# Joining two value products into one of 512 columns, squaring half rows in another order, and a place of its own for one tile of Fourier rows

## The chip, the core and the metric

The kernel runs on one core of a Trainium2 chip. The metric is the device time of one execution in microseconds (us), the median of several runs. The engines are named as the profile names them: PE (TensorE matmul) and PEld (its weight load), DVE (VectorE), ACT (ScalarE), POOL (GpSimd) and SP (SyncE, which here only issues DMAs). Instructions of one engine run in the order in which they stand in its queue.

## The reference, cut to what matters

One encoder layer for 512 + 256 tokens of width 2048: an RMS norm, an input projection, two groups of heads (a Fourier mix and windowed attention), an output projection, a squared-ReLU MLP and a last norm. What this case touches:

```python
h = rmsnorm(x, ln_mix_g)
z = h @ w_in                       # columns: 1024 Fourier | 1024 q | 256 k | 256 v
v = z[..., o3:].reshape(B, S, N_KV_HEADS, HEAD_DIM)
of = fourier_mix(zf, w_fourier).reshape(B, S, F_WIDTH)
mixed = concatenate([rmsnorm(of, out_norm_fourier_g), rmsnorm(oa, out_norm_attn_g)], -1)
x = x + mixed @ w_out
```

The inputs and results are float32.

## The kernel before, in words

**Products in parts.** Every float32 operand is split into a high and a low part (`split`, L66: ACT copies the source into the rounded high part, DVE subtracts it from the source for the low part), and a product is the sum of three matmuls: high by high, high by low, low by high.

**The value stage (L473 to L606)** is the first of the kernel. It makes v = x w for all 768 tokens (six tiles `m` of 128 rows) with 256 columns of `w_in[9]`, over 16 slices `k` of 128. `prepare(c)` scales and splits the x and w of one chunk: six chunks of one slice, then five of two slices. `v_term(c, m, term, i)` (L539) issues one matmul: stationary is a 128x128 block of x, moving are 256 columns of w, and the three terms of a tile add up in the first 256 columns of its PSUM bank `pv[m]`. The halves of w lie in two tiles, `whl[..][0]` (high) and `whl[..][1]` (low). In the last chunk the order is by tile, so that `pv[0]` is done first; `v_keep(m)` (L559) then splits `pv[m]` from PSUM into `vhl`, ACT first and DVE after it.

In the same stage `half_load(i)` (L548) reads six half rows of x (`halves[0]` to `halves[5]`, tiles named `xt`, 1024 columns each), and `half_square(i)` (L553) squares one on ACT and keeps its sum. Three of the six, 0 to 2, are squared after `high7(0)` and `high7(1)` and ahead of the six `v_keep`, the others, 3 to 5, after them. DVE has, in its order: `low7(0)`, `low7(1)`, two `xsum` (L404), the six subtractions of `v_keep`.

**The seven-product stage (L654 on)** follows at once. `product7(n)` (L276) issues 24 matmuls of 384 columns (L287) on weights which `load7(n)` (SP, L238) reads, `high7(n)` (ACT, L265) rounds and `low7(n)` (DVE, L273) completes; for each block of weights the third matmul is the first to use the low part. Products 0 and 1 use weights prepared in the value stage. `load7(2)` is the first to read into a tile named `wr`, and `high7(2)` stands on ACT right behind the squares of `halves`. Product 0 writes the PSUM banks of `pv[0]` and `pv[1]`, so it waits for the last reader of `pv[0]`.

**Where tiles lie.** The value stage's pool `xp` is closed before the pool `hq` of the next stage opens, and `hq` gets the same bytes of SBUF. A load into a new tile waits for the last instruction that reads or writes an old tile under it. In KB per partition from the start of both pools, as the program of the kernel before places them:

| pool | tile and place |
|---|---|
| `xp` | `wv[0..3]` 0-4, 12-16, 8-12, 4-8; `vt` 16-28 |
| `xp` | `halves[0]` 28-32, `[1]` 48-52, `[2]` 44-48, `[3]` 40-44, `[4]` 36-40, `[5]` 32-36 |
| `hq` | `ws` 0-24, `d7` 24-30, `z10` 30-34.5, `z01` 34.5-43.5 |
| `hq` | `wr` of `load7(2)` 43.5-47.5, of `load7(4)` 51.5-55.5, of `load7(6)` 47.5-51.5 |

**The Fourier rows.** `of_d` in DRAM holds the result of the Fourier group. `load_of(m)` (L180, its DMA L189) reads the 1024 rows of one tile m of tokens, `split_of(m)` (L1222) splits them for the output projection, and `proj_slot` (L1235) multiplies: 8 steps of k for each tile m, interleaved with attention by an order written out by hand. In that part `at(t, fn)` puts work at a step (slot m begins at 8 m), and the constants `t_...` (L1182 to L1186) are such steps. Before it, `after(piece, fn, place)` (L909) puts work behind a piece of the last input product (`pz`, L1001). `load_of(0)` reads early, into two tiles of the pool `kq2`; `load_of(1)` (L1248) stands behind the last piece and reads into the place of a later tile in the pool `op`, under which tiles of the pz stage lie.

Of the kernel before, what the change touches and what calls it, by code (L numbers as in the profile page):

```python
# [11 lines left out]
F32 = mybir.dt.float32  # L12
F32R = mybir.dt.float32r
BF16 = mybir.dt.bfloat16
AF = mybir.ActivationFunctionType
ALU = mybir.AluOpType
# [4 lines left out]
P = 128  # L21
# [4 lines left out]
NM = T // P  # L26
NK = D // P
# [4 lines left out]
NKV = 4  # L32
# [8 lines left out]
def hybrid_encoder(ctx: ExitStack, tc: tile.TileContext, a: dict):  # L41
    nc = tc.nc
# [156 lines left out]
    with ExitStack() as ph:  # L199
# [273 lines left out]
        with tc.tile_pool(name="xp", bufs=1, reuse_waits="tile") as xp, tc.manual_schedule(  # L473
            engines={mybir.EngineType.SP, mybir.EngineType.Activation, mybir.EngineType.DVE}
        ):

            wv = [xp.tile([P, 4, 256], F32, tag="raw", name="raw", bufs=4) for _ in range(4)]
            whl = [[wpool.tile([P, 4, 256], F32R, tag=t, name=t, bufs=4) for t in ("wh", "wl")] for _ in range(4)]
            flat = xs[1][:].rearrange("p o k t -> p (o k t)").rearrange("p (s o t) -> p s o t", s=8, o=2)
            vt = xp.tile([P, 4, 2, HALF], F32R, tag="vt", name="vt")  # L480
            room = [flat[:, 0:4], flat[:, 4:8], vt[:]]
            chunks = [(k, 1) for k in range(6)] + [(k, 2) for k in range(6, NK, 2)]
            homes = [(k // 4, k % 4) for k in range(6)] + [(1, 2), (2, 0), (0, 0), (1, 0), (2, 0)]
            xhl = {}

            def load_x(k0, n):
                for t in range(2):
                    nc.sync.dma_start(xr[k0 // 8][t][:, k0 % 8 : k0 % 8 + n, :], a["x_t"][:, t, k0 : k0 + n, :])

            def load_wv(k0, n, queue=nc.sync):  # L490
                queue.dma_start(wv[k0 // 4][:, k0 % 4 : k0 % 4 + n, :], w_in[9][:, k0 : k0 + n, :])

            def prepare(c):

                k0, n = chunks[c]
                r, s0 = homes[c]
                ks = slice(k0 % 8, k0 % 8 + n)
                raw = [xr[k0 // 8][t][:, ks, :] for t in range(2)]
                rows = [room[r][:, s0 + i * n : s0 + i * n + n] for i in range(2 if k0 >= 8 else 1)]
                if k0 < 8:  # L500
                    parts = [[xs[0][:, o, ks, :] for o in range(2)]]
                else:
                    parts = []
                parts += [[x[:, :, o, :] for o in range(2)] for x in rows]
                xhl[c] = parts
                w, wk = k0 // 4, slice(k0 % 4, k0 % 4 + n)
                wh, wl = (x[:, wk, :] for x in whl[w])
                gb = g0[:, k0 : k0 + n].rearrange("p (k o) -> p k o", o=1).to_broadcast([P, n, HALF])
                gain = lambda t: nc.vector.tensor_tensor(out=raw[t], in0=raw[t], in1=gb, op=ALU.mult)
                first = 1 if n == 1 else 0  # L510
                scaled = lambda k, out, x: nc.scalar.activation(out, x, AF.Copy, scale=g0[:, k : k + 1])
                if n == 1:
                    split(wh, wl, wv[w][:, wk, :])
                if c < 2:
                    for t in range(2):
                        split(*parts[t], raw[t], g0[:, k0 : k0 + 1])
                    return
                if n == 1:
                    scaled(k0, parts[0][0], raw[0])
                    gain(0)  # L520
                for i in range(n):
                    scaled(k0 + i, raw[first][:, i], raw[first][:, i])
                if n == 1:
                    nc.vector.tensor_tensor(out=parts[0][1], in0=raw[0], in1=f32(parts[0][0]), op=ALU.subtract)
                    split(*parts[1], raw[1])
                else:
                    gain(1)
                    split(wh, wl, wv[w][:, wk, :])
                    for t in range(2):
                        split(*parts[t], raw[t])  # L530
                if 6 <= c < 8:
                    k = c - 6
                    x, y = (xr[0][t][:, k, :] for t in range(2))
                    scaled(k, x, x)
                    nc.vector.tensor_scalar(out=y, in0=y, scalar1=g0[:, k : k + 1], scalar2=None, op0=ALU.mult)

            pv = [pp.tile([P, 512], F32, tag="x", bufs=6, name="pv") for m in range(NM)]

            def v_term(c, m, term, i):  # L539
                k0, n = chunks[c]  # L540
                l, r = ((0, 0), (0, 1), (1, 0))[term]
                k = k0 + i
                nc.tensor.matmul(  # L543
                    pv[m][:, :256], xhl[c][m // 3][l][:, i, m % 3 * P : (m % 3 + 1) * P], whl[k // 4][r][:, k % 4, :],
                    start=(k == 0 and term == 0), stop=(k == NK - 1 and term == 2),
                )

            def half_load(i):  # L548
                m, h = divmod(i, 2)
                halves[i] = xp.tile([P, 1024], F32, tag="xt", name="xt", bufs=6)[:]  # L550
                nc.sync.dma_start(halves[i], x_rows(m)[:, h * 1024 : (h + 1) * 1024])

            def half_square(i):  # L553
                m, h = divmod(i, 2)
                nc.scalar.activation(halves[i], halves[i], AF.Square, accum_out=ssq[:, 4 * m + h : 4 * m + h + 1])

            halves = {}

            def v_keep(m):  # L559
                split(vhl[:, m, :, 0, :], vhl[:, m, :, 1, :], pv[m][:, :256].rearrange("p (g d) -> p g d", g=NKV))  # L560

            pw = pp.tile([P, 512], F32, tag="t", bufs=2, name="pw")

            def warm(n):
                for _ in range(n):
                    nc.tensor.matmul(pw[:, :P], ones[:], ones[:], start=True, stop=True)

            warm(9)
            nc.scalar.dma_start(gall[:], a["gains"])
            nc.scalar.activation(mhalf[:, 7:8], mhalf[:, 7:8], AF.Copy)  # L570
            for k, n in ((0, 1), (1, 2), (3, 2), (5, 2), (7, 1), *((k, 2) for k in range(8, NK, 2))):
                if k % 2 == 0:
                    load_wv(k, 2)
                load_x(k, n)
                if k in (1, 3, 5):
                    load_wv(k + 1, 2)
            for i in range(2):
                half_load(i)
                load7(i)
            for i in range(2, 6):  # L580
                half_load(i)
            for c, (k0, n) in enumerate(chunks):
                prepare(c)
                if c + 1 < len(chunks):
                    order = [(term, m) for term in range(3) for m in range(NM)]
                    if n == 1:
                        order.sort(key=lambda x: (x[1] // 3, x))
                    for term, m in order:
                        for i in range(n):
                            v_term(c, m, term, i)  # L590
                else:
                    for n2 in range(2):
                        high7(n2)
                        low7(n2)
                    for i in range(3):
                        half_square(i)
                    for m in range(NM):
                        for term in range(3):
                            for i in range(n):
                                v_term(c, m, term, i)  # L600
            for n in range(2):
                xsum(b11, b12, b11, n)
            for m in range(NM):
                v_keep(m)
            for i in range(3, 6):
                half_square(i)  # L606

        def row_load(i):
# [234 lines left out]
        kt = {}  # L843
# [65 lines left out]
        def after(piece, fn, place=6):  # L909
            todo.setdefault(piece, []).append((place, len(todo[piece]), fn))  # L910
# [50 lines left out]
        after(7.5, close_folds, 7)  # L961
        after(8.5, close_fourier, 7)
        after(9, lambda: load_of(0, [kt["kq2"].tile([P, 4, P], F32, tag="ofr", name="ofr", bufs=2) for _ in range(2)]), 7)
        after(9, lambda: load_q(1), 8)
        after(10.5, lambda: load_q(2), 8)
        after(9, negate_sink, 8)
# [216 lines left out]
    t_trans, d_trans, t_th, t_tl, t_pv, d_pv, t_ob, t_os, t_put = 9.2, 1.05, 1.2, 1.4, 16.2, 0, 0.5, -0.6, 2.2  # L1183
    t_w, t_of, t_xc, t_y, t_oa, t_oa0, t_oa1, t_lq = 42.05, 7.45, -0.05, 2.7, 67, 4.2, 4.95, 1.5
    t_low = {2: 3.3}
    t_sq, t_red, t_w3, d_w, t_of1, t_of2, t_lof, t_la = 6.7, 7.9, 0.5, 2.15, 3, 6.5, 15.2, 1  # L1186
    events, clock = [], [0.0, 0]

    def at(t, fn):
# [55 lines left out]
                    nc.tensor.matmul(ps, ll(kk), pieces[kk // 2][0][:, kk % 2, :], start=False, stop=False)  # L1245
            step(k)

    load_of(1)  # L1248
    ofs = [[op.tile([P, FG, P], F32R, tag=f"of{c}{m}", name=f"of{c}{m}") for c in "hl"] for m in range(NM)]
    at(-2, lambda: split_of(0))  # L1250
    at(t_w3, lambda: out_split(3, False))
# [771 lines left out]
```

## Time and profile before

| | before |
|---|---|
| median of 3 runs | 2564.15 us (2563.36 to 2564.28) |
| the profiled execution, its time | 2563.83 us |
| its span in the profile | 2562.0 us |
| PE busy | 2552.0 us of the span |
| DVE / ACT / POOL busy | 1810.6 / 1127.7 / 272.6 us |
| mean granted clock of PE | 0.999 |

The profile shows one execution of 2563.83 us. Its rows begin with a start in us from the start of the span and a duration; several alike in a row are grouped as xN with the time from the first start to the last end. In square brackets stands the idle time before an instruction and what ended it. A matmul's duration contains its way through the array, so what one costs in a row of them is the distance from start to start.

### The profile page before, as it was taken

Reading aid. Unit: us, or ns where it says so; the run is one execution under the profiler, and the core shown is the slowest. Engines: PE = TensorE matmul, PEld = TensorE weight load, DVE = VectorE, ACT = ScalarE, POOL = GpSimd, SP = SyncE. Lnnn points to the kernel's source line nnn. Section 1 sums busy time; section 2 is a strip of 40 time slices with the busy share of each in tenths; the row PEclk is TensorE's granted clock in tenths of the full one; section 3 lists DMA queues with packets and bytes.
Section 4 is the critical chain, followed back from the end, with each engine's and each line's share of the span. In section 5 each row is a group of like instructions: output and inputs, shape, how many; then the busy total and the mean of one; then the engine's idle time right before and its main releaser. Section 6 shows DMA issues by size and latency. Waiting matters only on the chain.

```text
span 2562.0 us, 34695 instructions
## 1 busy us (share of the span) xinstructions
PE 2552.0 (100%) x13415; PEld 2336.7 (91%) x13415; DVE 1810.6 (71%) x2144; ACT 1127.7 (44%) x1630; POOL 272.6 (11%) x387
## 2 busy tenths in 40 slices
PE   9999999999999999999999999999999999999998
PEld 9999998888899999999999999988888888888887
DVE  7877767678466556556777777667766756777687
ACT  7454557674233333334445454433333333333335
POOL 0023333223201010100000000200000000000000
PEclk9999999999999999999999999999999999999999
DMA  7686386465745444466666666775543662554364
GB/s 294 229 285 214 115 245 193 138 179 187 236 163 186 159 165 163 165 207 225 231 230 214 217 215 216 277 279 176 176 146 124 221 222 89 176 183 157 101 211 153
DMA packets 261029, 496.99 MB, mean 194 GB/s; under 512 B 21147, under 2 KB 145569, under 8 KB 260737
## 3 DMA queue, kind: packets, MB, share of 16 engines
q1 hardware_dynamic: 193600, 332.00, 40.7%
q10 hardware_dynamic: 51360, 101.43, 10.5%
q0 software_dynamic: 15904, 61.36, 7.1%
q8 instruction: 105, 1.72, 0.3%
q14 instruction: 60, 0.48, 0.1%
HBM read 373.19 MB, written 121.51 MB: 193 GB/s over the span
## 4 chain that ended last, share of the span: by engine, by line
PE 98%; DMA 1%; DVE 0%; ACT 0%; issue 0%; POOL 0%; SPq 0%; ACTq 0%; DVEq 0%; POOLq 0%
PE pu L1390 36%; PE pd L1825 35%; PE pm L1243 10%; PE p L287 7%; PE pz L1001 3%; PE pv L543 1%; PE o L1122 1%; PE s L1045 1%; PE t L1100 1%; PE pa L796 0%; PE ptx L138 0%; PE pe L815 0%; DMA ofd<-of 0%; DMA raw<-in_w_out 0%; DMA xr<-in_x_t 0%
## 5 line engine op out<-in xcount | busy, mean ns | idle before, releaser
L1390 PE MATMUL pu<-xf,wh 128*128 128x384 f32 x3072 | 780.2, 334 | 0.0
L1390 PEld LDWEIGHTS pu<-xf,wh 128*128 128x128 f32 x3072 | 554.1, 188 | 1.5 <-ACT o L1408 1.3
L1825 PE MATMUL pd<-wh,sh 128*128 128x512 f32 x1332 | 517.7, 389 | 0.0
L1825 PE MATMUL pd<-wl,sh 128*128 128x512 f32 x1332 | 517.7, 389 | 0.0
L1825 PE MATMUL pd<-wh,sl 128*128 128x512 f32 x1332 | 517.5, 389 | 0.0
L1390 PE MATMUL pu<-xf,wl 128*128 128x384 f32 x1536 | 513.1, 334 | 0.0
L1802 ACT ACTIVATE wh<-rd 128x1024 fp32r<-128x1024 f32 x200 | 202.4, 1054 | 522.3 <-PE pd L1825 424.4
L1812 DVE TENSOR_TENSOR wl<-rd,wh 128x1024 fp32r<-128x1024 f32 x200 | 236.1, 1221 | 226.2 <-ACT wh L1802 225.5
L1370 ACT ACTIVATE wh<-ur 128x1024 fp32r<-128x1024 f32 x160 | 170.1, 1063 | 382.6 <-PE pu L1390 226.7
L1825 PEld LDWEIGHTS pd<-wl,sh 128*128 128x128 f32 x1332 | 250.0, 188 | 51.9
L1825 PEld LDWEIGHTS pd<-wh,sh 128*128 128x128 f32 x1332 | 250.0, 188 | 51.9
L1825 PEld LDWEIGHTS pd<-wh,sl 128*128 128x128 f32 x1332 | 249.9, 188 | 51.8 <-DVE sl L1813 0.3
L1390 PEld LDWEIGHTS pu<-xf,wl 128*128 128x128 f32 x1536 | 288.3, 188 | 0.0
L1376 DVE TENSOR_TENSOR wl<-ur,wh 128x1024 fp32r<-128x1024 f32 x160 | 195.5, 1222 | 76.1 <-ACT wh L1370 76.1
L1411 DVE TENSOR_TENSOR o<-pu,o 128x768 f32<-128x768 f32 x160 | 152.9, 956 | 122.4 <-PE pu L1390 114.9
L287 PE MATMUL p<-xs,wh 128*128 128x384 f32 x672 | 170.6, 334 | 0.0
L1795 DVE TENSOR_TENSOR rd<-rd 128x1024 f32<-128x1024 f32 x112 | 131.7, 1217 | 0.0
L1390 PE MATMUL pu<-xs,wh 128*128 128x384 f32 x512 | 129.8, 334 | 0.0
L1370 ACT ACTIVATE wh<-sx 128x1024 fp32r<-128x1024 f32 x64 | 67.9, 1062 | 130.5 <-PE pu L1390 104.3
L287 PEld LDWEIGHTS p<-xs,wh 128*128 128x128 f32 x672 | 121.4, 188 | 0.1
L287 PE MATMUL p<-xs,wl 128*128 128x384 f32 x336 | 112.2, 334 | 0.0
L1813 DVE TENSOR_TENSOR sl<-sr,sh 128x768 fp32r<-128x768 f32 x111 | 105.6, 951 | 0.0
(309 smaller groups left out, 3774.9 us busy)
## 6 DMA issues: line engine op xcount, KB each, us to landing
rd<-in_w_down SPq DMA_DIRECT2D x176, 512.0 KB, 5.2
ur<-in_w_up SPq DMA_DIRECT2D x128, 512.0 KB, 3.8
sr<-sd SPq DMA_DIRECT2D x95, 384.0 KB, 5.4
pd<-o ACTq DMA_DIRECT2D x60, 384.0 KB, 2.3
o<-pd POOLq DMA_DIRECT2D x60, 384.0 KB, 6.2
sd<-sm ACTq DMA_DIRECT2D x60, 384.0 KB, 2.8
raw<-in_w_in SPq DMA_DIRECT2D x40, 512.0 KB, 5.1
raw<-in_w_out SPq DMA_DIRECT2D x32, 512.0 KB, 4.5
```

The lines of the kernel that those rows point to most:

```text
L287: nc.tensor.matmul(ps7[own, g, r][:, :HALF], l[:, i, r * P : (r + 1) * P], x[:, o, 4 * e + i, :], start=(opens and e == 0 and i == 0 and q ...
L1001: nc.tensor.matmul(ps[c][s][:, :HALF], w[:, i, cs], whole[j // 2][s][o][:, 4 * (j % 2) + i, :], start=first and n == 0, stop=stop and n == 2,)
L1243: nc.tensor.matmul(ps, l(k), w[:, k % 2, :], start=(k == 0 and n == 0), stop=(k == 7 and n == 2))
L1370: nc.scalar.activation(wh[:], raw[:], AF.Copy)
L1376: nc.vector.tensor_tensor(out=wl[:], in0=raw[:], in1=f32(wh[:]), op=ALU.subtract)
L1390: nc.tensor.matmul(ps[:, t, :HALF], w[:, i, t * P : (t + 1) * P], xb[:, o, i, :], start=(s == first_of[bank] and i == 0 and n == 0), stop= ...
L1411: nc.vector.tensor_tensor(out=o, in0=src, in1=o, op=ALU.add)
L1795: add = lambda x, y, op: nc.vector.tensor_tensor(out=x[:], in0=x[:], in1=y[:], op=op)
L1802: nc.scalar.activation(wh[:], t[:], AF.Copy)
L1812: nc.vector.tensor_tensor(out=wl[:], in0=t[:], in1=f32(wh[:]), op=ALU.subtract)
L1813: nc.vector.tensor_tensor(out=sl[:], in0=sr[:], in1=f32(sh[:]), op=ALU.subtract)
L1825: nc.tensor.matmul(o, l[:, q, ts], w[:, ns], start=(j == j0 and (q, t) == (0, 0)), stop=(j == j1 and (q, t) == (1, 2)),)
```

## The change

1. **Joined value products.** `whl` is laid out so that the high and the low part of one slice lie side by side (512 columns). Term 0 multiplies the high part of x by both at once (512 columns, into the whole bank `pv[m]`), term 1 the low part of x by the high part of w (256 columns). A tile and slice now takes two matmuls instead of three. A new `v_sum(m)` adds the two halves of the bank: ACT copies the second 256 columns into `wv[m // 2]`, DVE adds the first 256. All six `v_sum` come ahead of the six `v_keep`, which now read from SBUF.
2. **Squares in another order.** `halves[3]` to `[5]` are squared ahead of the last chunk's end, `halves[0]` to `[2]` behind the six `v_keep`.
3. **`load_of(1)`** is issued behind piece 9.5 instead of behind the last piece, into two tiles of its own (`ofn`, 2 KB per partition each) in `kq2`. `split_of(1)` so works on two tiles, and its step is 4.4 (8 - 3.6) instead of 5 (8 - 3).

```diff
-            whl = [[wpool.tile([P, 4, 256], F32R, tag=t, name=t, bufs=4) for t in ("wh", "wl")] for _ in range(4)]
+            whl = [wpool.tile([P, 2, 2, 256], F32R, tag=t, name="whl", bufs=4) for _ in range(4) for t in ("wh", "wl")]
...
-                wh, wl = (x[:, wk, :] for x in whl[w])
+                wh, wl = (whl[k0 // 2][:, k0 % 2 : k0 % 2 + n, o, :] for o in range(2))
...
             def v_term(c, m, term, i):
                 k0, n = chunks[c]
-                l, r = ((0, 0), (0, 1), (1, 0))[term]
                 k = k0 + i
+                w = whl[k // 2][:, k % 2, : 2 - term, :].rearrange("p o c -> p (o c)")
                 nc.tensor.matmul(
-                    pv[m][:, :256], xhl[c][m // 3][l][:, i, m % 3 * P : (m % 3 + 1) * P], whl[k // 4][r][:, k % 4, :],
-                    start=(k == 0 and term == 0), stop=(k == NK - 1 and term == 2),
+                    pv[m][:, : 512 - 256 * term], xhl[c][m // 3][term][:, i, m % 3 * P : (m % 3 + 1) * P], w,
+                    start=(k == 0 and term == 0), stop=(k == NK - 1 and term == 0), skip_group_check=term > 0,
                 )
...
+            def v_sum(m):
+                t = wv[m // 2][:, m % 2, :]
+                nc.scalar.activation(t, pv[m][:, 256:], AF.Copy)
+                nc.vector.tensor_tensor(out=t, in0=pv[m][:, :256], in1=t, op=ALU.add)
+
             def v_keep(m):
-                split(vhl[:, m, :, 0, :], vhl[:, m, :, 1, :], pv[m][:, :256].rearrange("p (g d) -> p g d", g=NKV))
+                split(vhl[:, m, :, 0, :], vhl[:, m, :, 1, :], wv[m // 2][:, m % 2, :].rearrange("p (g d) -> p g d", g=NKV))
...
-                    order = [(term, m) for term in range(3) for m in range(NM)]
+                    order = [(term, m) for term in range(2) for m in range(NM)]
...
-                    for i in range(3):
+                    for i in range(3, 6):
                         half_square(i)
                     for m in range(NM):
-                        for term in range(3):
+                        for term in (1, 0):
                             for i in range(n):
                                 v_term(c, m, term, i)
             for n in range(2):
                 xsum(b11, b12, b11, n)
             for m in range(NM):
+                v_sum(m)
+            for m in range(NM):
                 v_keep(m)
-            for i in range(3, 6):
+            for i in range(3):
                 half_square(i)
...
+        after(9.5, lambda: load_of(1, [kt["kq2"].tile([P, 4, P], F32, tag="ofn", name="ofr", bufs=2) for _ in range(2)]), 6)
...
-    t_sq, t_red, t_w3, d_w, t_of1, t_of2, t_lof, t_la = 6.7, 7.9, 0.5, 2.15, 3, 6.5, 15.2, 1
+    t_sq, t_red, t_w3, d_w, t_of1, t_of2, t_lof, t_la = 6.7, 7.9, 0.5, 2.15, 3.6, 6.5, 15.2, 1
...
-    load_of(1)
```

## The prediction

> **What bounds the kernel now.** I read the page first, then the chain of waits in order of time, then the timelines of PE, ACT, DVE and SP around the two places of the change.
>
> ```profile
> span 2562.0 us, 34695 instructions
> PE 2552.0 (100%) x13415; PEld 2336.7 (91%) x13415; DVE 1810.6 (71%) x2144; ACT 1127.7 (44%) x1630; POOL 272.6 (11%) x387
> ```
>
> PE is idle for 10 us of 2562. So an edit can help only by taking time out of PE's own row of matmuls or out of those few waits, and it hurts wherever PE must wait for a part not yet ready. The chain gives what a matmul costs in a long row:
>
> ```profile
> 40.93 120.65 PE p L287 x696
> ...
> 1639.82 906.07 PE pd L1825 x3996
> ```
>
> 384 columns take 120.65 / 696 = 173.3 ns, 512 columns 906.07 / 3996 = 226.7 ns. The value stage, from PE's timeline:
>
> ```profile
> 20.61 1.60 PE L543 MATMUL pv<-wl,xs 128*128 128x256 f32 x12
> 22.05 1.60 PE L543 MATMUL pv<-wh,xs 128*128 128x256 f32 x12
> ...
> 40.53 0.40 PE L543 MATMUL pv<-wh,vt 128*128 128x256 f32 x2
> 40.77 0.51 PE L287 MATMUL p<-xs,wh 128*128 128x384 f32 x2
> ```
>
> Twelve matmuls of 256 columns start within 22.05 - 20.61 = 1.44 us: 120 ns each. Product 0 begins at 40.77 with no gap. Each matmul has about 13.3 ns beside its columns (226.7 - 120 = 106.7 for 256 more).
>
> **1. Joining.** 96 pairs of 2 x 120 become 96 matmuls of 226.7: 96 x 13.3 = 1.28 us less on PE. That is the upper bound; V would end between 39.5 and 40.77. Preparation keeps up in the main, since both DVE and ACT have already gone on to work of the next stage (DVE's `xsum` at 36.43 below, ACT's squares ahead of 37.76 in part 3) while PE still works on V.
>
> What can be kept of it is set by DVE. The rows of DVE:
>
> ```profile
> 36.43 3.42 DVE L404 TENSOR_TENSOR xr<-xr,xr 128x1536 f32<-128x1536 f32 x2
> 39.77 2.07 DVE L70 TENSOR_TENSOR vhl<-pv,vhl 128x256 fp32r<-128x256 f32 x6
> 47.38 1.23 DVE L273 TENSOR_TENSOR wl<-wr,wh 128x1024 fp32r<-128x1024 f32 x1 [5.54 <-ACT wh L265]
> 50.05 1.76 DVE L410 TENSOR_TENSOR xs<-xr,xs 128x1536 fp32r<-128x1536 f32 x1 [1.44 <-ACT xs L407]
> 51.73 1.22 DVE L273 TENSOR_TENSOR wl<-raw,wh 128x1024 fp32r<-128x1024 f32 x1
> ...
> 54.53 1.22 DVE L273 TENSOR_TENSOR wl<-wr,wh 128x1024 fp32r<-128x1024 f32 x1
> ```
>
> and from the groups of instructions, with mean ns of one:
>
> ```profile
> L70 DVE TENSOR_TENSOR vhl<-pv,vhl 128x256 fp32r<-128x256 f32 x6 | 2.1, 410 | 0.0
> ```
>
> DVE goes from its `xsum` straight to the first reader of `pv[0]`, at 39.77, whatever PE does. After the change that reader is the addition of `v_sum(0)`, of the same shape (0.41 us): the bank of `pv[0]` is free at 40.19, and product 0 can start at about 40.24, as soon as V has ended at all. So joining gives 40.77 - 40.24 = **0.53 us**; the other 0.75 us turn into a wait for DVE. Without that wait it would be 1.28, which I keep for the range; no less than 0 if V's operands came late.
>
> The Trainium skill, page "TensorE: Matmul & The Clock Gate", section "Back-to-back issue gap", puts an isolated gap at N / 2.4 + 2.5 ns. By that rule joining would save only 2.5 ns a pair, an estimate of 0.24 us in all, and it speaks against this edit; the rows above (120 and 226.7 ns) show 13.3, so I go by the rows. (In the first rival below, that rule would give 2563.83 - 0.24 = 2563.6 in place of 2563.3.)
>
> **2. v_sum and v_keep.** Six ACT copies (0.38 us each in the row of 40.97 below) and six DVE additions are new, in front of `v_keep`. ACT is free at 37.76, so the copies of tiles 0 to 4 lie beside V's end. DVE: additions start 0.33 apart ((2.07 - 0.41) / 5), so the sixth ends at 39.77 + 2.07 = 41.84. `v_keep`'s last ACT copy needs it: it starts at 41.88 instead of 40.97. DVE's six subtractions end near 44, in time that was idle (5.54 us before 47.38). What pays is ACT's queue behind: everything after `v_keep` moves by 0.91 us.
>
> **3. The squares.** This is the term that decides. ACT and SP:
>
> ```profile
> 37.76 0.71 ACT L69 ACTIVATE vhl<-pv 128x256 fp32r<-128x256 f32 x2
> ...
> 40.97 0.38 ACT L69 ACTIVATE vhl<-pv 128x256 fp32r<-128x256 f32 x1 [0.34 <-PE pv L543]
> 41.25 1.05 ACT L555 ACTIVATE xt<-xt 128x1024 f32<-128x1024 f32 x1
> 42.20 0.19 ACT L555 ACTIVATION_READ_ACCUMULATOR xt<-xt 128x1 f32 x1
> ...
> 44.28 0.19 ACT L555 ACTIVATION_READ_ACCUMULATOR xt<-xt 128x1 f32 x1
> 46.29 1.06 ACT L265 ACTIVATE wh<-wr 128x1024 fp32r<-128x1024 f32 x1 [1.82 <-DMA wr<-in_w_in]
> ```
>
> ```profile
> 42.42 0.33 SPq L238 DMA_DIRECT2D wr<-in_w_in  x1
> 42.84 0.38 SPq L238 DMA_DIRECT2D raw<-in_w_in  x1
> 43.27 0.43 SPq L238 DMA_DIRECT2D wr<-in_w_in  x1
> ```
>
> `load7(2)` goes out at 42.42, right behind the end of the fourth square, `halves[3]`, at 42.20 + 0.19 = 42.39; the load at 43.27 waited for none of the later ones. That agrees with the table of places: `wr` of `load7(2)`, 43.5 to 47.5 KB, lies over the end of `halves[3]` and over most of `halves[2]`. Before, `halves[2]` was squared ahead of `v_keep`. In the new order it is the last of all six. So moving `halves[3]` forward does not free the load: it now waits for `halves[2]`.
>
> When is that? The last `v_keep` copy at 41.88, the first late square 0.28 later (41.25 - 40.97) at 42.16, three squares take 44.47 - 41.25 = 3.22: end at 45.38, load out at 45.41, 3.0 us later than 42.42. What hangs on it moves by the same 3.0: the landing, `high7(2)` 49.3 to 50.35, `low7(2)` until 51.6; SP's loads behind it too, so `high7(3)`, the `xs` step behind it on ACT, and `low7(3)`, until 51.73 + 1.22 + 3.0 = 55.95; `low7(4)` until 58.75.
>
> PE: product 0 at 40.24, two products of 24 x 0.1733 later, 48.56, product 2 is due; its third matmul at 48.91. It gets its low part at 51.65: **2.74 us** of stall. Product 3's third matmul would be due at 51.65 + 24 x 0.1733 = 55.81, and waits for 55.99: **0.18**. Where product 2 resumes is set by the load alone: had joining gained nothing, the stall would be 0.53 shorter and the sum the same. Product 4's third is due at 60.15, 1.4 us after its low part: PE is ahead of nothing any more, and the rest follows as before, later by the sum. The early squares of `halves[3]` to `[5]` take the slots of the others, up to 37.76; the transfers are over by then, as DMA falls to almost nothing at 35 us:
>
> ```profile
> 30.00:35.00 5.00, 5.00 (x44) 5.00 (x43) 5.00 (x7) 4.92 (x8) 0.00 (x0) 1.00 0.91 365
> 35.00:41.00 6.00, 6.00 (x52) 6.00 (x51) 6.00 (x8) 4.66 (x12) 0.00 (x0) 1.00 0.02 7
> ```
>
> (The last two columns are the DMA share and GB/s.)
>
> **4. load_of(1).** Before:
>
> ```profile
> 345.98 4.13 SPq L79 DMA_DIRECT2D raw<-in_w_out  x2
> 352.74 0.55 SPq L189 DMA_DIRECT2D ofr<-ofd  x1
> 359.56 1.04 ACT L1226 ACTIVATE ofh<-ofr 128x1024 fp32r<-128x1024 f32 x1
> 360.11 0.40 PE L1045 MATMUL s<-kd,qs 128*128 128x256 f32 x2
> 360.66 0.50 PE L1243 MATMUL pm<-wh,ofh 128*128 128x512 f32 x1 [0.15 <-ACT ofh L1226]
> 359.35 0.68 DVE L340 TENSOR_TENSOR zs<-zs,cosr 128x512 f32<-128x512 f32 x1
> 360.74 1.22 DVE L1227 TENSOR_TENSOR ofl<-ofr,ofh 128x1024 fp32r<-128x1024 f32 x1
> 364.68 1.14 DVE L1088 TENSOR_SCALAR p<-p,rs 128x256 f32<-128x256 f32 x4
> 366.30 0.60 PE L1100 MATMUL t<-ident,p 128*128 128x128 f32 x4
> ```
>
> SP has a gap between its two `raw` loads, into which the two new DMAs (0.5 us of issue each) fall; the second `raw` and `load_q(2)` then queue behind 512 KB more. PE waits at 360.66 for the first part of `ofh`: two short matmuls before it take 0.24, so about 0.3 us of the 0.55 are a stall. Split in two, the first half would be ready about 0.4 earlier: a gain of 0.3. Against it, DVE's order turns: at step 4.4 the two subtractions stand ahead of the rotation at 359.35 (step 4.8) and wait for ACT's first half until about 360.2. DVE runs without a gap there, so up to 0.85 us of delay reach the scaling of `p` at 364.68 (ends at 365.82), which PE needs at 366.30, 0.5 later: a stall of up to 0.7. I take **0**, with -0.3 and +0.7 as ends.
>
> **The sum**, against the profiled execution's 2563.83: -0.53 + 2.74 + 0.18 + 0 = +2.4, so 2566.2 us. That execution lies 0.32 below the median and inside the runs shown, so I add no correction. A measurement of this kernel tells about 0.2%, 5.1 us, from no change: this is 0.09%, no change, on its slow side.
>
> **The rivals.**
>
> *The load is not held by `halves[2]`* (places differ after the change, or the wait names another tile): the load goes out right after the early squares, ACT reaches `high7(2)` at 45.4 at the latest, its low part is done near 47.7 and product 2, due at 48.56, waits for nothing. Then 2563.83 - 0.53 = 2563.3, and with the 0.3 of part 4 2563.0: faster than before, by less than can be told. For it: the order looks made to free `wr`. Against it: the table, and the row at 42.42.
>
> *The whole 1.28 arrives* and with it 0.3: 2562.2. For it stands only that DVE's queue might run ahead; against it, DVE works without a gap up to 39.77.
>
> *The stall cascades, slower by over 5.1 us.* Place: products 3 and 4, fed through the same SP queue. Price: each us by which the late load lands later than the 3.87 us of before (42.42 to 46.29) adds to the stall in full. It decides from a landing of about 6.6 us: then 2.4 + 2.7 = +5.1, 2569. Against it: DMA is nearly idle there.
>
> **How the numbers follow.** Forecast (2565.2 to 2567.6): 0.66. Load not held, and the whole gain: 0.22 together (2562.2 to 2563.5). Cascade or another stall beyond 2567.6: 0.10, of which half above 2569. Gain beyond 5.1 us: 0.02; I see no row that could give it. The range 2562.4 to 2567.8 leaves out some 0.15. Faster by over 0.2% 0.02, within 0.2% 0.93, slower 0.05.
>
> **What would show it.** 96 fewer matmuls in the page (13319). Product 0 near 40.2, behind a wait for DVE. The first `wr` load near 45.4, behind the last square, and PE's wait in front of product 2, about 2.7 us, on `high7(2)` and `low7(2)`. V itself shorter by 1.0 to 1.3 us. Around 360, a shorter wait on `ofh` and a later scaling of `p`. I am wrong if the first `wr` load goes out before 42, if product 2 starts without a wait, or if the time moves by more than 4 us.

## The result, and the profile after

| | before | after |
|---|---|---|
| median | 2564.02 us (16 runs, 2562.54 to 2565.74) | 2569.76 us (16 runs, 2568.19 to 2573.3) |
| the profiled execution, its span | 2563.83, 2562.0 us | 2570.19, 2568.4 us |

The ratio is 1.0024, with a 95% interval of 1.0017 to 1.0031: slower by 5.7 us. The forecast was 2566.2, and the time lies above its range.

The page after shows 96 matmuls fewer and PE idle for 14.6 us in place of 10:

```profile
span 2568.4 us, 34531 instructions
PE 2553.8 (99%) x13319; PEld 2332.0 (91%) x13319; DVE 1811.2 (71%) x2151; ACT 1129.2 (44%) x1637; POOL 272.2 (11%) x387
```

PE has five new waits in the changed kernel: 1.74 us for `wh` and 0.64 for `wl` ahead of product 2, 0.83 for `z` ahead of product 8 (their rows stand below), and at the start of attention one for `qs` and one for the `ofh` of the first tile. The 0.15 for the `ofh` of the second tile is gone. The list of PE's waits has the two of attention as follows (us in total, times, longest):

```profile
PE s L1053 <- DMA qs<-ql: 1.3, 1, 1.3
...
PE pm L1251 <- ACT ofh L1234: 0.6, 1, 0.6
```

Where the waits act is read from the chain after (start, duration, what):

```profile
2.58 5.85 DMA xr<-in_x_t
...
11.27 29.02 PE pv L543 x165
40.69 1.84 ACT vhl L69 x6
42.52 3.13 ACT xt L555 x6
...
61.65 7.95 DMA raw<-in_w_in
...
77.81 87.73 PE p L287 x504
165.65 54.09 PE p L287 x312
...
372.38 3.04 DMA ql<-zs
376.66 4.57 DMA qs<-ql
...
1646.22 906.04 PE pd L1832 x3996
```

The chain before had no DMA and no ACT piece between 11 and 161 us:

```profile
11.16 29.77 PE pv L543 x246
...
161.69 54.09 PE p L287 x312
```

The last block of p starts at 165.65 in place of 161.69: **3.96 us** are lost in the value and product stages. The last stage, `pd`, starts at 1646.22 in place of 1639.82, 6.40 later. So another **2.44 us** are lost between, and the rows put them at the start of attention: the first `s` that needs the queries read back from DRAM starts 215.71 us behind the last block of p in place of 213.35.

PE's timeline after, around product 0, and its waits with the last matmul ahead of them:

```profile
40.34 0.62 PE L287 MATMUL p<-xs,wh 128*128 128x384 f32 x2
...
48.60 0.34 PE L287 MATMUL p<-xs,wl 128*128 128x384 f32 x1
50.68 0.62 PE L287 MATMUL p<-xs,wh 128*128 128x384 f32 x2 [1.74 <-ACT wh L265]
51.94 0.44 PE L287 MATMUL p<-xs,wl 128*128 128x384 f32 x1 [0.64 <-DVE wl L273]
...
76.64 0.34 PE L287 MATMUL p<-xs,wl 128*128 128x384 f32 x1
77.81 0.62 PE L287 MATMUL p<-xs,wh 128*128 128x384 f32 x2 [0.83 <-ACT z L308]
```

A matmul takes 0.1733 us from start to start, so product 2 was due at 48.60 + 0.17 = 48.77 and came 1.91 us later. Its third matmul was due at 51.03 and came 0.91 later: together 2.82. Product 8 was due at 76.81 and came 1.00 later. In the kernel before it started at 74.06:

```profile
74.06 0.51 PE L287 MATMUL p<-xs,wh 128*128 128x384 f32 x2
```

So PE's delay was 2.75 us when it reached product 8 (76.81 less 74.06) and 3.75 from there on. SP (first fence) and ACT (second) show the load that holds product 2, ACT and DVE (third) the sums that hold product 8:

```profile
45.67 0.33 SPq L238 DMA_DIRECT2D wr<-in_w_in  x1
```

```profile
45.46 0.18 ACT L555 ACTIVATION_READ_ACCUMULATOR xt<-xt 128x1 f32 x1
49.57 1.06 ACT L265 ACTIVATE wh<-wr 128x1024 fp32r<-128x1024 f32 x1 [3.92 <-DMA wr<-in_w_in]
...
74.94 1.06 ACT L265 ACTIVATE wh<-ws 128x1024 fp32r<-128x1024 f32 x1 [2.50 <-DVE ws L257]
75.91 1.47 ACT L407 ACTIVATE xs<-xr 128x1536 fp32r<-128x1536 f32 x1
77.28 0.47 ACT L308 ACTIVATE z<-p 128x384 f32<-128x384 f32 x1
```

```profile
60.39 1.22 DVE L257 TENSOR_TENSOR ws<-wr,raw 128x1024 f32<-128x1024 f32 x1 [0.28 <-DVE wl L273]
64.75 1.23 DVE L257 TENSOR_TENSOR ws<-wr,raw 128x1024 f32<-128x1024 f32 x1 [0.72 <-DMA raw<-in_w_in]
69.68 1.23 DVE L257 TENSOR_TENSOR ws<-wr,raw 128x1024 f32<-128x1024 f32 x1 [0.90 <-DMA raw<-in_w_in]
73.63 1.22 DVE L257 TENSOR_TENSOR ws<-wr,raw 128x1024 f32<-128x1024 f32 x1
```

The same four sums of the kernel before, on DVE:

```profile
57.24 1.23 DVE L257 TENSOR_TENSOR ws<-wr,raw 128x1024 f32<-128x1024 f32 x1 [0.35 <-DMA raw<-in_w_in]
61.34 1.23 DVE L257 TENSOR_TENSOR ws<-wr,raw 128x1024 f32<-128x1024 f32 x1 [0.46 <-DMA raw<-in_w_in]
65.28 1.22 DVE L257 TENSOR_TENSOR ws<-wr,raw 128x1024 f32<-128x1024 f32 x1
69.23 1.22 DVE L257 TENSOR_TENSOR ws<-wr,raw 128x1024 f32<-128x1024 f32 x1
```

The load goes out 3.25 us later (45.67 for 42.42), and the sums run later by 3.15, 3.41, 4.40 and 4.40. PE was later by only 2.75. So the copy that empties the bank for product 8, which ACT does behind these sums, came later than PE did, and PE had to wait once more.

At the start of attention DVE's rows after read:

```profile
364.79 1.29 DVE L1235 TENSOR_TENSOR ofl<-ofr,ofh 128x512 fp32r<-128x512 f32 x2 [0.79 <-ACT ofh L1234]
366.00 0.68 DVE L340 TENSOR_TENSOR zs<-zs,cosr 128x512 f32<-128x512 f32 x1
368.00 0.68 DVE L340 TENSOR_TENSOR zs<-zs,cosr 128x512 f32<-128x512 f32 x1
```

The second rotation of the queries started at 362.48 before; 368.00 less the 3.96 is 364.04, so it is 1.56 later. These queries go to DRAM and are read back (the two pieces of the chain at 372.38 and 376.66), and PE waits 1.3 us for `qs` behind them.

### The profile page after: what moved, and what is told of

Same layout as the page of the kernel before. It is cut to its first block, busy times and chain, and to the rows that moved or that the text cites. A ratio compares the mean times of both kernels' runs of the same rounds, so it can differ in the third digit from the quotient of the medians.

```text
span 2568.4 us, 34531 instructions
## 1 busy us (share of the span) xinstructions
PE 2553.8 (99%) x13319; PEld 2332.0 (91%) x13319; DVE 1811.2 (71%) x2151; ACT 1129.2 (44%) x1637; POOL 272.2 (11%) x387
## 4 chain that ended last, share of the span: by engine, by line
PE 95%; DMA 2%; DVE 1%; ACT 1%; issue 0%; SPq 0%; POOL 0%; ACTq 0%; DVEq 0%; POOLq 0%
PE pu L1397 36%; PE pd L1832 35%; PE pm L1251 10%; PE p L287 6%; PE pz L1009 3%; PE pv L543 1%; PE o L1130 1%; PE s L1053 1%; PE t L1108 1%; DMA raw<-in_w_in 1%; PE pa L803 0%; PE ptx L138 0%; PE pe L822 0%; DMA ofd<-of 0%; DMA ofr<-ofd 0%
```

## Experiments

All differences are a few us of 2564, and single runs of one kernel spread by about 1 us either way. So each kernel is judged by two things: the difference of the mean times to the runs of before that were taken with it (its interval in brackets is by resampling these runs), and where its one profile shows the time. By the wider interval of the ratio (0.0009 either side, 2.3 us) only the changed kernel, `e1` and `g1` differ from before for certain. "Last p" is the start of the last block of p, in the chain. `e2` leaves everything ahead of the last p as it was, so its 0.24 us earlier load and 0.32 later last p show how far two profiles differ by themselves.

| kernel | what it is | first `wr` load at | last p at | time against before, us |
|---|---|---|---|---|
| before | | 42.42 | 161.69 | |
| after | parts 1, 2, 3 | 45.67 | 165.65 | +6.2 (5.4 to 6.9) |
| e1 | parts 1, 2 | 45.53 | 165.42 | +4.4 (3.9 to 4.8) |
| e2 | part 3 | 42.18 | 162.01 | +1.6 (1.3 to 2.0) |
| e3 | part 2 | 44.23 | 164.41 | +2.1 (1.6 to 2.6) |
| e4 | part 1 | 43.54 | 163.73 | +1.9 (1.3 to 2.7) |
| e5 | after, squares 1, 2, 3 early | 37.70 | 161.10 | +1.1 (0.5 to 1.7) |
| e6 | part 1, squares 1, 2, 3 early | 37.71 | 161.08 | -0.1 (-0.6 to 0.5) |

### The two losses apart: e1 and e2

`e1` is the changed kernel with this edit:

```diff
-        after(9.5, lambda: load_of(1, [kt["kq2"].tile([P, 4, P], F32, tag="ofn", name="ofr", bufs=2) for _ in range(2)]), 6)
...
-    t_sq, t_red, t_w3, d_w, t_of1, t_of2, t_lof, t_la = 6.7, 7.9, 0.5, 2.15, 3.6, 6.5, 15.2, 1
+    t_sq, t_red, t_w3, d_w, t_of1, t_of2, t_lof, t_la = 6.7, 7.9, 0.5, 2.15, 3, 6.5, 15.2, 1
...
+    load_of(1)
```

> The changed kernel with part 3 undone: load_of(1) again behind the last piece, at its old place, and its split at step 5 again; joining and the new order of squares stay. Theory (two separate losses): the value and product stages lose 4.0 us as in the changed kernel (last block of p at 165.6 in place of 161.7), and no more is lost at the start of attention: the first s behind the rotated queries goes on at its old distance, no wait of PE for qs. Span 2562.0 + 4.0 = 2566.0, time about 2567.8. Rival (the second loss follows from the lateness of the first stage, not from load_of(1)): the wait for qs stays and the span is about 2568.4 again.

Measured: median 2568.26, ratio 1.0017 (1.0008 to 1.0026), span 2566.6, last p at 165.42; no wait for `qs`. The loss is not quite at an end there, as the theory had it: behind the last p the profile loses another 0.84 us, with a wait of 0.96 for `nm` (a value for each row that DVE makes in attention). `e2` is the kernel before with the opposite edit.

> The kernel before with part 3 alone: load_of(1) behind piece 9.5 in two tiles of its own, split at step 4.4. Theory: the stages up to the last p keep their times (last block of p at 161.7), and the start of attention loses 2.4 us, with a wait of about 1.3 us of PE for qs and 0.6 for the first ofh. Span 2562.0 + 2.4 = 2564.4. Rival (part 3 costs nothing by itself, as I had predicted): span 2562.0 within 0.3, no wait for qs.

Measured: median 2565.13, ratio 1.0006 (0.9997 to 1.0016), span 2564.0, a wait of 0.48 for `qs`. Within their intervals the two losses are separate and add up: 4.4 + 1.6 = 6.0 of 6.2. In time part 3 costs less than the one profile of the changed kernel had shown (2.4).

### The first loss is the order of the squares: e5 and e3

`e5`, against the changed kernel:

```diff
-                    for i in range(3, 6):
+                    for i in (1, 2, 3):
                         half_square(i)
...
-            for i in range(3):
+            for i in (0, 4, 5):
                 half_square(i)
```

> The changed kernel with another choice of squares: 1, 2 and 3 ahead of the end of the value stage, 0, 4 and 5 behind v_keep, so that no late square reads a tile that lies under the first wr. Theory (the order of squares alone makes the first loss): the first wr load goes out ahead of 40 in place of 45.67, PE waits neither ahead of product 2 nor of product 8, the last block of p starts near 161.3 in place of 165.65, and the span is 2568.4 - 4.4 = 2564.0; the 2.4 at the start of attention stay. Rival (v_sum, with its six new copies and six new additions, pushes high7(2) and what follows back whatever the load does): the load goes out early, and PE still waits 1 us or more ahead of products 2 to 8; span 2566 or more.

Measured: median 2564.94, span 2564.6. The first load goes out 8 us earlier, and no wait of PE from product 2 on remains; the chain holds one piece from product 0 to the last block of p:

```profile
40.05 120.94 PE p L287 x696
161.10 54.09 PE p L287 x312
```

By the means 5.1 us go with the choice of three tiles (3.8 by the two spans, 4.55 by the start of the last p). `v_sum`, which stands in `e5` as in the changed kernel, is not what costs there. `e3` is the kernel before with `range(3, 6)` early and `range(3)` late:

> The kernel before with the new order of squares alone (3 to 5 early, 0 to 2 behind v_keep). Theory: halves[2] is the last square, the first wr load goes out at 44.5 in place of 42.4; its low part comes at about 50.7 where product 2 needs it at 49.4, so PE stalls 1.3 there, and 0 to 1.3 more at product 8 if the delay comes back through the loads; span 2563.4 to 2564.6. Rival (the late load matters only together with v_sum): span 2562.0 within 0.3.

Measured: median 2565.8, span 2563.8. Two of PE's four waits in this stage of `e3` (the others are 0.29 ahead of product 2 and 0.44 at 55.43):

```profile
50.55 0.45 PE L287 MATMUL p<-xs,wl 128*128 128x384 f32 x1 [0.64 <-DVE wl L273]
...
76.46 0.61 PE L287 MATMUL p<-xs,wh 128*128 128x384 f32 x2 [0.30 <-ACT z L308]
```

The load is 1.81 later than before, and the stage 2.7: more than the lateness itself, here too with a second wait at product 8.

### Joining: e4, e6 and f1

`e4` is part 1 alone, `e6` part 1 with squares 1, 2, 3 early.

> The kernel before with part 1 alone: joined products, v_sum ahead of v_keep, squares in their old order (0 to 2 early, 3 to 5 late). Theory (joining gives 0.4 to 0.5 us, and v_sum takes most of it back because the first late square, halves[3], over which the first wr lies, moves back by 0.9): product 0 starts 0.4 earlier than in the kernel before, the first wr load goes out at 43.3, PE waits 0.3 to 0.6 ahead of product 2's low part, the last block of p starts at 161.5 to 162.3 (161.7 before), span 2561.8 to 2562.8. Rival (v_sum itself is what costs): a wait of over 1 us ahead of products 2 to 8, span 2563.5 or more.

Measured: median 2565.82, span 2565.0. The load went out where expected, at 43.54; what I missed is again the second wait:

```profile
49.76 0.45 PE L287 MATMUL p<-xs,wl 128*128 128x384 f32 x1 [0.49 <-DVE wl L273]
75.50 0.62 PE L287 MATMUL p<-xs,wh 128*128 128x384 f32 x2 [0.71 <-ACT z L308]
```

So `v_sum` does cost in the old order of squares (last p 2.04 later), and since `e6` below has the same `v_sum` without this loss, it is not by its work but by the 1.1 us by which it moves the square of `halves[3]`, and with it the load. The other 0.9 us of the span of `e4` lie in attention, behind a wait of 1.53 for `ofh`, whose read landed late, in a stage that this edit leaves alone.

> The kernel before with part 1 and with squares 1, 2 and 3 early, 0, 4 and 5 late; no part 3. Theory: the gain of joining is kept, no wait ahead of products 2 and 8, the last block of p starts at 161.1 to 161.3, no wait for qs, span 2561.0 to 2562.0 (2562.0 before), time 0.4 to 0.7 below the kernel before. Rival (the whole change costs by its added work on ACT and DVE): span 2563 or more.

Measured: median 2564.13, span 2561.8, last p 0.61 earlier than before. The expected gain of 0.4 to 0.7 did not come: the time is that of before, and the profile has a wait of 1.38 for `ofh`. `f1` is `e6` with DVE's order turned:

```diff
-            for n in range(2):
-                xsum(b11, b12, b11, n)
-            for m in range(NM):
+            xsum(b11, b12, b11, 0)
+            for m in range(2):
+                v_sum(m)
+            xsum(b11, b12, b11, 1)
+            for m in range(2, NM):
                 v_sum(m)
```

> e6 (joined products; squares 1, 2, 3 early; no part 3) with another order on DVE: v_sum(0) and v_sum(1) stand between the two xsum of 1.75 us, not behind both. Theory (in the joined kernels product 0 waits 0.85 us for the bank of pv[0], which DVE's v_sum(0) holds): product 0 starts at 39.2 to 39.4 in place of 40.05 with no gap ahead of it, the last block of p at 160.2 to 160.6 in place of 161.08, no wait ahead of products 2 and 8, and the time falls by 0.7 to 0.9 against e6, so about 2563.3 against 2564.1 of the kernel before. Rival (product 0 is held by something else, the end of V or its weights): it starts at 40.05 again and the time is that of e6.

Measured: median 2564.29 against 2564.36 of before, span 2562.5. The wait ahead of product 0 is gone, yet product 0 starts at 39.99, only 0.06 earlier than in `e6`, where 0.7 was expected. PE's rows of `f1`:

```profile
35.80 4.35 PE L543 MATMUL pv<-whl,vt 128*128 128x256 f32 x24
39.99 0.51 PE L287 MATMUL p<-xs,wh 128*128 128x384 f32 x2
```

The last 24 matmuls take 12 x 0.2267 + 12 x 0.12 = 4.16 us and end at 39.96. V itself ends there, and in `e6`, by the same count, at 39.82: the wait on the bank was 0.23 us, not 0.85, and the rest was V's own late end. The time is missing ahead of 11.2 us, where the chain of both kernels runs through the arrival of x and its preparation (after: the 5.85 us of `xr` from 2.58 on, then ACT and DVE): at 11.16 before had 42 of its 288 matmuls behind it (14 of 96 sets), at 11.27 after had 27 of 192 (13.5 of 96). From there on V takes 29.02 for 29.77, a gain of 0.75.

### The second wait: g1

The changed kernel with one copy on ACT moved ahead:

```diff
-            step(high_at, 6 + 2 * e, lambda e=e: xhigh(h0, b11, e))
+            step(high_at, 5 + 3 * e, lambda e=e: xhigh(h0, b11, e))
```

> The changed kernel with one ACT copy of 1.47 us (xhigh of the next x, L407) moved from behind high7(9) to behind high7(8), so that it no longer stands ahead of the copy that empties the bank for product 8. Theory (the second stall, 1.0 us ahead of product 8, is the ACT queue: the bank's copy stands behind high7(9), which waits for the late sum, and behind this copy): the bank's copy ends near 76.4 in place of 77.7, PE's wait ahead of product 8 falls from 1.0 to 0.1 or less, the last block of p starts 0.9 earlier (164.7), the time is 0.9 below that of the changed kernel. Rival (PE is held by the transfers themselves, the queue only names it): product 8 starts on time and the same 1 us is lost ahead of products 9 to 12; last block of p at 165.6 again.

Measured: median 2569.9, span 2567.7, last p at 165.98. The rival holds: product 8 starts on time, and half a product later PE waits 1.10 us, where the changed kernel had waited 0.83. PE's and ACT's rows of `g1`:

```profile
80.28 0.61 PE L287 MATMUL p<-xs,wh 128*128 128x384 f32 x2 [1.10 <-ACT z L308]
```

```profile
78.80 1.06 ACT L265 ACTIVATE wh<-ws 128x1024 fp32r<-128x1024 f32 x1 [2.23 <-DVE ws L257]
79.76 0.47 ACT L308 ACTIVATE z<-p 128x384 f32<-128x384 f32 x1
```

The copy that empties the bank stands behind `high7`, and `high7` waits 2.23 us for a late sum. So the 1.47 us copy set only the place of the wait; what stays is the row of late sums.

### What in part 3 costs: e7, e8, f2, g2, h1, h3, h2

Part 3 has two halves: the read goes out earlier (**transfer**), and the split moves from step 5 to 4.4 (**order**). `e7` is the transfer alone on the kernel before, `e8` the order alone:

```diff
-    t_sq, t_red, t_w3, d_w, t_of1, t_of2, t_lof, t_la = 6.7, 7.9, 0.5, 2.15, 3, 6.5, 15.2, 1
+    t_sq, t_red, t_w3, d_w, t_of1, t_of2, t_lof, t_la = 6.7, 7.9, 0.5, 2.15, 3.6, 6.5, 15.2, 1
```

> The kernel before with the early load_of(1) into two tiles of its own, but split at its old step 5. It tells the transfer from the order on DVE. Theory (the order does it: the two subtractions stand ahead of the rotation at step 4.4): the rotation of the first queries keeps its distance, no wait of PE for qs over 0.3; what is left is what the early transfer costs, a wait of 0 to 0.6 for the first wh or ofh; span 2562.0 to 2562.6. Rival (the early transfer pushes out_load(2) and load_q(2) back and that does it): the wait for qs stays, 0.5 to 1.5, span 2563 to 2564.4.

> The kernel before with the split of the second tile at step 4.4 alone; load_of(1) at its old place, in one tile. Theory (the order on DVE does it): the subtraction waits ahead of the rotation for ACT's copy, which ends near 360.6, so the rotation of 359.35 moves to about 361.8, the queries are stored and read about 2.4 later, and PE waits for qs 1.5 to 2.4; span 2563.5 to 2564.5. Rival (the early transfer does it): no wait for qs, span 2562.0 within 0.5.

Measured: `e7` median 2565.04, +0.7 (0.1 to 1.4), a wait of 0.81 for `qs` in its profile (span 2562.8); `e8` median 2565.59, +1.1 (0.5 to 1.8), although the one profile, taken in its shortest run (2563.83), shows 0.17. Neither theory alone. `f2` is `f1` with the read behind `load_q(2)`, `g2` the same with the order:

```diff
         after(10.5, lambda: load_q(2), 8)
+        after(10.5, lambda: load_of(1, [kt["kq2"].tile([P, 4, P], F32, tag="ofn", name="ofr", bufs=2) for _ in range(2)]), 9)
...
-    load_of(1)
```

> The same, and the rows of the second tile in a place of their own, but read behind out_load(3) and load_q(2) (after piece 10.5) and split at the old step 5. Theory (what made part 3 dear was that its 512 KB were put ahead of out_load(3) and load_q(2), and that the split was put ahead of the rotation): without both, the rows lie ready in time, PE's wait of 0.3 to 1.5 for the ofh of the second tile goes, the wait for qs is at most 0.3, and the time falls by 0.3 to 1.0 against the other kernel of this call. Rival (any early read of these rows delays what PE needs at the start of attention): 0.5 to 1.5 slower than it.

> f2 (rows of the second tile in their own place, read behind load_q(2)) with the split at step 4.4 in place of 5. It tells what the order on DVE costs by itself. Theory (the subtractions ahead of the rotation hold the queries back): the first rotation starts 1.0 to 2.5 later, the second up to 1.1 later, PE waits for qs by 0.3 to 1.0 more, the time is 0.5 to 1.5 above f2. Rival (the order costs nothing as long as the read is not ahead of out_load(3)): the time is that of f2 within 0.4, and PE's wait for the second tile's ofh is shorter.

Measured: `f2` median 2563.84, -0.5 (-1.2 to 0.2), `g2` median 2564.11, +0.1 (-0.5 to 0.8). `f2` is not told from before or from `f1`. The last three stand on `f1` and ran on one chip, each against the runs of before there (`f1` itself ran on another): `h1` with the read behind piece 9.5, `h3` with step 4.4, `h2` with both.

> f1 (no stall in the value and product stages, time about that of the kernel before) with load_of(1) early, behind piece 9.5, split at step 5. Theory (the early 512 KB stand ahead of out_load(3) and load_q(2) and share the transfers with out_load(2)): 0.5 to 1.2 above f1; the wh copies behind out_load(2) and out_load(3) start 1.5 to 2 later, the second rotation at about 362.9 on the clock of the kernel before, and PE waits for qs by 0.5 to 1.0. Rival (only the order on DVE costs): within 0.3 of f1.

> f1 with the split of the second tile at step 4.4 alone, the read at its old place. Theory (the order costs as much as the transfer): 0.5 to 1.2 above f1, the first rotation 1.5 to 2.5 later, the second 0.5 to 1. Rival (the second rotation, which sets the queries, stands behind the same subtraction either way, so the order costs nothing): within 0.3 of f1.

> f1 with the whole of part 3. Theory (transfer and order do not add up, since both delay the same second rotation): 1.1 to 1.8 above f1, the second rotation at 364.0 to 364.5, PE waits for qs by 0.5 to 1.6. Rival (they add up): the sum of the two others.

Measured: `h1` median 2563.96, -0.1 (-0.7 to 0.4); `h3` 2564.47, +0.8 (0.2 to 1.4); `h2` 2564.9, +1.0 (0.4 to 1.6). `h1` came out as its rival had it, and `h2` has no wait for `qs`, which its theory asked for. DVE's rows of `h1`, then of `h2`, whose last blocks of p start at 161.03 and 161.05:

```profile
358.51 0.68 DVE L340 TENSOR_TENSOR zs<-zs,cosr 128x512 f32<-128x512 f32 x1
359.90 1.29 DVE L1237 TENSOR_TENSOR ofl<-ofr,ofh 128x512 fp32r<-128x512 f32 x2
361.70 0.68 DVE L340 TENSOR_TENSOR zs<-zs,cosr 128x512 f32<-128x512 f32 x1
```

```profile
359.67 1.29 DVE L1237 TENSOR_TENSOR ofl<-ofr,ofh 128x512 fp32r<-128x512 f32 x2 [0.79 <-ACT ofh L1236]
360.88 0.69 DVE L340 TENSOR_TENSOR zs<-zs,cosr 128x512 f32<-128x512 f32 x1
362.88 0.68 DVE L340 TENSOR_TENSOR zs<-zs,cosr 128x512 f32<-128x512 f32 x1
```

In the old order the first rotation fills the time in which ACT makes `ofh`. In the new one DVE stands idle for 0.79 us, and the second rotation comes 1.18 later. The order was exchanged in five pairs (e8 to before, h3 to f1, g2 to f2, h2 to h1, e2 to e7), and each time the mean rose: by 1.1, 0.8, 0.6, 1.1 and 0.9 us. Taken singly, the first and the last two are clear of zero; together they make 0.9 (0.6 to 1.2). The transfer, in four pairs (e7 to before, h1 to f1, h2 to h3, e2 to e8), made 0.7, -0.2, 0.2 and 0.5, together 0.3 (-0.1 to 0.7), which these runs don't tell from nothing.

The path by which the order costs is shown only in part. Counted from the last p, the second rotation is later in each of the five pairs, by 0.5 to 1.5 us, and so is the first `s` that needs its queries, by 0.2 to 1.0. But PE's wait at this `s` names `qs` in `e8`, `h3` and `e2` only. In `g2` and `h2` it names `nm` of DVE, and `e7` and `h1` wait for `qs` (0.81 and 0.35) in the old order too. How much of the 0.9 goes by way of `qs` stays open.

## Why the prediction was wrong, step by step

**1. Joining (0.53 expected).** Product 0 starts 0.43 earlier (40.34 for 40.77), so the size held: as expected, DVE sets this start, when it has read `pv[0]` at 39.87 + 0.41 = 40.28. The division behind it did not hold. I had V end early and wait 0.75 for DVE. V's last matmuls end at about 40.07 and the wait is 0.27: the step "preparation keeps up in the main" failed, because the first 11 us of V are set by the arrival of x and its preparation. I had read the rows of 20 to 40 us only. The Trainium skill, page "TensorE: Matmul & The Clock Gate", section "Back-to-back issue gap", gives 2.5 ns beside the columns of an isolated matmul, which for the 82 sets behind 11 us makes an estimate of 0.2 us; measured are 0.75 (29.77 for 29.02), for half a set more of work. This trace does not agree with it, as the rows of before did not. By the 13.3 ns that the prediction had read from its own rows, 82 sets gain 1.09 us, and half a set more of work takes 0.17 of it back: 0.92, with 0.75 measured.

**2. `v_sum` and `v_keep`.** On ACT the first late square starts at 42.43 where I had 42.16. `v_keep`'s six copies follow each other there from 40.58 without a gap, so ACT itself and not the sixth addition sets them: 0.27 more.

**3. The squares (2.74 + 0.18).** This step held nearly to the digit: the load at 45.67 (45.41), waits of 2.82 ahead of product 2 (2.74) and about 0.15 around product 3's third matmul (0.18). What failed is the sentence "the rest follows as before, later by the sum". The loads, the roundings, the low parts and the sums form a ring, in which each load waits for a buffer that the sum before it frees (the load of 61.65 goes out behind the sum that ends at 60.39 + 1.22 = 61.61). This ring moved by 3.15 and then by 4.4 us, while PE had moved by 2.75. In the kernel before the bank of product 8 was emptied at 73.35, 0.7 ahead of its use at 74.06 (ACT's row):

```profile
72.88 0.47 ACT L308 ACTIVATE z<-p 128x384 f32<-128x384 f32 x1
```

4.4 less 0.7 is 3.7, which is PE's delay from then on (3.75). I had checked product 4 and no further. That the ring moved by 4.4 and not by 3.25 comes from a landing: the load of 61.65 took 7.95 us. Its counterpart before went out at 58.49 and had landed by 65.28, within 6.8. Why it took one more here is not shown, but the DMA engines are full at that time in both kernels (a share of 0.99 in the kernel before from 62 to 66 us). Of the changed kernel (the last two columns are the DMA share and GB/s):

```profile
42.00:46.00 4.00, 4.00 (x25) 4.00 (x24) 1.95 (x6) 3.64 (x8) 0.00 (x0) 1.00 0.00 0
...
66.00:70.00 4.00, 4.00 (x25) 4.00 (x24) 3.10 (x3) 1.44 (x2) 0.54 (x1) 1.00 1.00 385
```

Nothing is read from 42 to 46 us, and from 58 to 70 us, where the share is 0.97 to 1.00, there is no spare rate with which to catch up. The Trainium skill, page "Trainium Kernel Development and Optimization", section "Key Constraints", says that the transfers of the SP, ACT and POOL queues run on the same 16 engines and interleave. The 7.95 us, twice the 3.87 of the first `wr` load of before, agree with that, though no run here shows which transfers took the time. I had named a cascade as a rival, but at products 3 and 4 and with a slow landing of the first load as its price; that load landed in 3.90 (45.67 to 49.57), as before. The cascade came without it, and at product 8. What I held against it, "DMA is nearly idle there", was a wrong reading: it holds from 35 to 41 us, but from 46 to 50 us the kernel before has a DMA share of 1.02 at 396 GB/s.

**4. `load_of(1)` (0 taken, -0.3 to +0.7).** Measured: 1.6 alone, about 0.9 of it for the order, the rest not told from nothing. I had seen that DVE's order turns and by how much (up to 0.85), but I followed the delay to the scaling of p, which had 0.5 to spare, and not to the rotation right behind the subtractions. In the changed kernel it goes on from there through ACT, a store and a read to PE's `s`, which waits 1.3 us for `qs`; over the pairs of runs only the cost of the order is shown, and this path in part. It is the term of the sum that was set at 0. The stall on the second tile's `ofh`, worth 0.3, did go, but PE now waits 0.63 us for the first tile's, which the prediction did not have.

**The sum.** By the means the change costs 6.2 us, and the sum had 2.4. Of the 3.8 that are missing, 1.6 lie ahead of the last p (3.96 in place of 2.39): 1.0 is the second wait, 0.1 comes from joining, and the other 0.5 are small, most of them slower rows behind a wait. Part 3 makes another 1.6. The last 0.6 is not assigned; it is within the intervals of the means, and `e1` too, without part 3, lost 0.84 in attention in its profile. The chance for slower by over 0.2% was set at 0.05; the step that made it too small is "PE is ahead of nothing any more, and the rest follows as before".

## What to carry to other kernels

When a load is held back, do not stop at the first product that waits for it. Where loads, roundings and sums form a ring through a few buffers and the DMA engines are full, the ring can be later than the load that set it back (4.4 for 3.25 us here); compare its delay with that of PE at every later place where PE takes something from it. And when the order on an engine is turned, follow every instruction behind the one that now waits, first of all those whose results leave for DRAM and come back.

To lay a new tile over an old one ties its load to the last reader of the old tile. Choosing which reader comes last (squares 1, 2, 3 early in place of 3, 4, 5) was worth 5 us here, more than joining was to gain (1.28 at most).

## What the runs showed that I had not expected

- The same stretch of program lands its loads differently from run to run: the 512 KB of `e1`'s load at 59.91 took 5.51 us, the changed kernel's at 60.14 about 4.6. In `e2` the second sum waited 1.34 us for its load where before it waited 0.46, and product 8 came 0.2 late (74.01 for 73.81), with nothing changed there: the kernel before has so little to spare at this place that the scatter reaches PE. One profile is therefore a weak witness for a loss of 1 us.
- Behind a wait PE's first two matmuls take 0.62 us in place of 0.51 (50.68 and 77.81 above; in `f1`, without a wait, 0.51 at 39.99), some 0.1 us on top of each wait.
- At the start of attention the distance from the last block of p to the first `s` that needs the rotated queries varied from 212.4 (`e3`) to 214.1 us (`e4`) without part 3. In `e6` and `f1` the last p was 0.6 to 0.8 us earlier than before and the time was the same; their profiles wait longer in attention (1.38 for `ofh`, 0.65 for `nm`), so such a gain need not reach the end.
